# Transposed products in a decoder trunk: two weight blocks at a time, sixteen matmuls with high parts, then sixteen with low parts

## The chip, the cores and the metric

The kernel runs on one core of a Trainium2 chip. Its time is the device time in microseconds (us), lower is better. A core has a matrix engine (PE, or TensorE), VectorE (DVE), ScalarE (ACT), GpSimd (POOL) and SyncE (SP), which in this kernel only issues transfers. The engines run side by side, each through its own row of instructions in order, and wait for one another by semaphores.

## The reference

Two decoder layers over 256 positions of width 2048, all in float32. Layer 0 mixes with a gated DeltaNet, layer 1 with sparse attention; each is followed by a convolutional gated feed-forward part (ffn, width 5120), layer norms and a per-layer embedding.

```
def conv_glu(x, w_gate, w_up, conv_w, w_down):
    gate = causal_dwconv(x @ w_gate, conv_w)
    return (jax.nn.silu(gate) * (x @ w_up)) @ w_down
...
    for i in range(DEPTH):
        if i % N_MIXERS == 0:
            h = gdn_mixer(x, gdn_w_in[ia], gdn_conv_w[ia], ...)
        else:
            h = dsa_mixer(x, dsa_w_in[ib], ...)
        x = layer_norm(DN_ALPHA * x + h, ln1_g[i], ln1_b[i])
        f = conv_glu(x, ffn_w_gate[i], ffn_w_up[i], ffn_conv_w[i], ffn_w_down[i])
        x = layer_norm(DN_ALPHA * x + f, ln2_g[i], ln2_b[i])
        x = x + jax.nn.sigmoid(x @ ple_w_gate[i]) * (p[i] @ ple_w_proj[i])
```

The DeltaNet works in chunks of 64 positions. In each, a triangular matrix made of keys and gates is inverted by forward substitution:

```
    lmat = jnp.where(strict, jnp.einsum('bhncd,bhnsd->bhncs', kb, k) * decay, 0.0)
    amat = lmat + jnp.eye(C, dtype=jnp.float32)
    sol = lax.linalg.triangular_solve(amat, rhs, left_side=True, lower=True, unit_diagonal=True)
```

Nearly all arithmetic is in products of the 256 positions with weight matrices of 2048 or more rows.

## The kernel before

**Products by parts.** PE keeps float32 exactness by splitting every operand in a high part (rounded to the format that PE multiplies in) and a low part (the rest). A product is then high x high, high x low and low x high. The activation is held turned, `xT`: 128 partitions, 16 row blocks, 2 parts, 256 positions. Weights come in blocks of 128 x 1024 elements (512 KB). For each block `weights` (lines 97 to 118) takes a buffer `raw` out of three (pool `wp`), issues its load on SP (line 104), lets ACT copy it into `hi` (line 110) and VectorE subtract into `lo` (line 111). `hi` and `lo` come from the pool `hl`, three buffers each (line 70). Both splits are issued with a priority far ahead, so the scheduler puts them as early as buffers allow.

**Transposed products** (`gemm_t_steps`, lines 120 to 143) have the weights as stationary operand and give their result turned, 128 columns on the partitions. For 256 columns they take two accumulators in PSUM and four blocks. In each block, eight matmuls with high parts (line 133) have high and low parts of the activation side by side as the moving operand (512 wide); then eight with low parts of the weights (line 137) have the high part of the activation alone (256 wide). After each block the generator yields, so that a caller can put other work between blocks; after the last one `done` takes the accumulators. They make the keys, queries and values of the DeltaNet (256 and 512 columns for each of eight groups of four heads; lines 453, 454 and 569), its gates (64 columns: one block of sixteen and sixteen, line 322), gate and up of the ffn (lines 736, 737), and in the sparse layer the index heads, keys and queries (lines 909, 938, 954, 986). The other products (`gemm_steps`, lines 145 to 169) have the activation as stationary operand; all their matmuls move weights (lines 161, 162, 165). They are not touched.

**Group 0 of the DeltaNet** is where other engines' chains matter. Its steps in order:
- the gates' product, turned back by `ab_ps` (line 326); some twenty small steps on VectorE and ACT (lines 328 to 343); `gc_ps` (lines 354 to 356) sums them over a chunk on PE;
- `grow` (line 361): these sums go to memory by POOL's queue; `qd` (line 434): SP loads them back, spread over all partitions; `L` (lines 443, 444): decays, on VectorE;
- `L` times the products of keys (line 513); `lt` (line 518) and `ld` (line 521): SP turns the triangular blocks by way of memory;
- `substitute` (lines 529 to 543): 62 small operations on POOL, then `tt` (line 543) and `pm` (line 557) bring the inverses back in place; `w_ps` (from `mul`, line 549) is PE's first use of them.

`lt` and `ld` share SP's queue with the loads of weights, which wait for `raw` buffers there. The later groups go through the same chain one group ahead, while PE works on products of the group before.

**What sets the order.** A scheduler puts instructions in each engine's row by priority and by what they depend on, from the order in which the program issues them; buffers of a pool are reused in turn.

Of the kernel before, what the change touches and what calls it, by code (L numbers as in the profile page):

```python
# [16 lines left out]
P = 128  # L17
S = 256
D = 2048
KT = D // P  # L20
# [43 lines left out]
class Trunk:  # L64
    def __init__(self, nc, tc, ctx, t):
        self.nc, self.tc, self.t = nc, tc, t
        pool = lambda **k: ctx.enter_context(tc.tile_pool(**k))

        self.const = pool(name="const", bufs=1)
        self.hl = pool(name="hl", bufs=3)  # L70
        self.xtp = pool(name="xtp", bufs=1)
        self.big = pool(name="big", bufs=1)
        self.cp = pool(name="cp", bufs=1, side="right")
        self.wp = pool(name="wp", bufs=3, side="right")
        self.mm = pool(name="mm", bufs=4, space=PSUM)
        self.sp = pool(name="sp", bufs=2, space=PSUM)
        self.dr = pool(name="dr", bufs=2, space=DRAM)
        self.ident = self.const.tile([P, P], F32, tag="ident", name="ident")
        nc.sync.dma_start(out=self.ident, in_=t["cst"][:, C_IDENT:C_IDENT + P])
        cst = self.cst = self.cp.tile([P, N_CONST - P], F32, tag="cst", name="cst")  # L80
        self.tri = cst[:, C_TRI - P:C_TRI - P + P]
        self.cmin = cst[:, C_CMIN - P:C_CMIN - P + P]
        self.xinit = cst[:, C_XINIT - P:C_XINIT - P + 256]
        self.ones = cst[:, C_ONES - P:C_ONES - P + P]
        self.causal = cst[:, C_CAUSAL - P:C_CAUSAL - P + P]
        self.qmin = cst[:, C_QMIN - P:C_QMIN - P + P]
        self.xT = self.xtp.tile([P, KT, 2, S], F32R, tag="xT", name="xT")
        self.behind, self.first = [], ()
# [28 lines left out]
            self.first = ()  # L117
        return hi, lo

    def gemm_t_steps(self, src, c0, n, x, done, kt=KT):  # L120


        nc = self.nc
        for c in range(c0, c0 + n, 256):
            w = min(256, c0 + n - c)
            nt = [(o, min(P, w - o)) for o in range(0, w, P)]
            ps = [self.mm.tile([P, 512], F32, tag="mm", name="mm_ps") for _ in nt]
            nk = 1024 // w
            for k0 in range(0, kt, nk):
                hi, lo = self.weights(src, k0 * P, nk, (c, w))  # L130
                for k in range(nk):
                    for (o, m), q in zip(nt, ps):
                        nc.tensor.matmul(q[:m, :], hi[:, k, o:o + m], x[:, k0 + k].rearrange("p a b -> p (a b)"),  # L133
                                         start=k0 + k == 0, stop=False)
                for k in range(nk):
                    for (o, m), q in zip(nt, ps):
                        self.tail = nc.tensor.matmul(q[:m, S:], lo[:, k, o:o + m], x[:, k0 + k, 0, :],  # L137
                                                     start=False, stop=k0 + k == kt - 1)
                if k0 + nk < kt:
                    yield  # L140
            for (o, m), q in zip(nt, ps):
                done((c - c0 + o) // P, q[:m, :])
            yield
# [38 lines left out]
            steps = [g for g in steps if next(g, steps) is not steps]  # L182

    def gemm_t(self, *args):
        self.go_(self.gemm_t_steps(*args))

    def gemm(self, *args):
        self.go_(self.gemm_steps(*args))
# [209 lines left out]
    def gdn_groups(self, pool, gk, cw, ng, oT, load, taps, gates, ahead):  # L398
# [4 lines left out]
        nc, t = self.nc, self.t  # L403
        w_in = t["gdn_w_in"]
# [10 lines left out]
        def conv(n0, out):  # L415

            def done(n, ps):
                pd = pads[n % 2]
                self.fold(pool, pd[:, 3:], ps)
                ac = pool.tile([P, S], F32, tag="ac", name="ac", bufs=2)  # L420
                w = cw[:, :, n0 + n]
                nc.scalar.activation(ac, pd[:, 3:], AF.Identity, scale=w[:, 3:4])
                for k in (2, 1, 0):
                    nc.vector.scalar_tensor_tensor(ac, pd[:, k:k + S], w[:, k:k + 1], ac, op0=ALU.mult, op1=ALU.add)
                o = out(n)
                nc.scalar.activation(o, ac, AF.Tanh, scale=0.5)
                nc.vector.scalar_tensor_tensor(o, o, 1.0, ac, op0=ALU.add, op1=ALU.mult)
            return done
# [19 lines left out]
        def keys(g, rest=()):  # L448

            s = {"g": g}  # L450
            q = s["q"] = pool.tile([P, 2, S], F32, tag="q", name="q")
            k = s["k"] = pool.tile([P, 2, S], F32, tag="k", name="k")
            steps = (self.gemm_t_steps(w_in, 2048 + 256 * g, 256, self.xT, conv(16 + 2 * g, lambda n: k[:, n])),
                     self.gemm_t_steps(w_in, 256 * g, 256, self.xT, conv(2 * g, lambda n: q[:, n])))
            if not g:

                for nb in range(4):
                    load(nb, self.tail if nb else None)
                    if nb:
                        next(steps[1])  # L460
                    if nb == 3:
                        taps(self.tail)
                    self.first = self.halves
                    next(steps[0])
                next(steps[1])
                gates()
            for x in steps:
                for _ in x:
                    if rest:
                        rest.pop(0)()  # L470
            return s
# [180 lines left out]
        def front(s):  # L652
            decays(s)
            sums(s)
            blocks(s)

        n, rest = keys(0), []
        front(n)
        substitute(n)
        for g in range(8):  # L660
            s = n
            rest += values(s)
            if g:
                zgate(s, rest)
                rest = []
            else:
                zgate(s, [])
            if g < 7:
                n = keys(g + 1, rest)
            else:  # L670
                ahead()
            inverses(s)
            if g < 7:
                front(n)
                substitute(n)
            solve(s)
            rest = outputs(s)
# [29 lines left out]
    def ffn(self, i, affine):  # L707
        nc, tc, t = self.nc, self.tc, self.t
        with tc.tile_pool(name="hp", bufs=1) as hp, tc.tile_pool(name="fp", bufs=1) as pool:
            NF = D_FF // P  # L710
            hT = self.parted(hp, "hT", NF)
            cw = self.fcw
            gates = {}
            pads = [pool.tile([P, 2 + S], F32, tag=f"fpd{i}", name=f"fpd{i}") for i in range(2)]
            for pd in pads:
                nc.gpsimd.memset(pd[:, 0:2], 0.0)

            def gate(n, ps):
                pd = pads[n % 2]
                self.fold(pool, pd[:, 2:], ps)  # L720
                ac = gates[n] = pool.tile([P, S], F32, tag="fac", name="fac", bufs=3)
                nc.scalar.activation(ac, pd[:, 2:], AF.Identity, scale=cw[:, 2, n:n + 1])
                for k in (1, 0):
                    nc.vector.scalar_tensor_tensor(ac, pd[:, k:k + S], cw[:, k, n:n + 1], ac,
                                                   op0=ALU.mult, op1=ALU.add)
                self.mark = nc.scalar.activation(ac, ac, AF.Silu)

            def up(n, ps):
                h = pool.tile([P, S], F32, tag="fh", name="fh", bufs=2)
                self.fold(pool, h, ps)  # L730
                nc.vector.tensor_tensor(h, h, gates[n], op=ALU.mult)
                self.split(hT(n)[:, 0], hT(n)[:, 1], h)

            distances = self.distances(pool) if not i else iter(())
            for n in range(0, NF, 2):
                steps = (self.gemm_t_steps(t["ffn_w_gate"][i], n * P, 256, self.xT, lambda m, ps: gate(n + m, ps)),
                         self.gemm_t_steps(t["ffn_w_up"][i], n * P, 256, self.xT, lambda m, ps: up(n + m, ps)))
                if n:
                    for x in steps:
                        self.go_(x)  # L740
                else:
                    self.go_(*steps)
                if n % 4 == 0:
                    next(distances, None)
                if n in (6, 14, 22, 30):
                    affine(pool, n // 8, self.mark)()
            return self.project(pool, t["ffn_w_down"][i], hT, NF, t["ln2_g"][i], t["ln2_b"][i], lambda: self.fill)
# [300 lines left out]
```

## Time and profile before

| what | value |
|---|---|
| three runs | 2846.52, 2847.19, 2851.07 us |
| median | 2847.19 us |
| span of the profiled execution, first to last instruction | 2843.5 us |
| ACT's splits (line 110), 929 of them | 977.8 us, 1053 ns each |
| loads over the span | 513.94 MB read, 183 GB/s |
| POOL's substitution, both lines, 248 operations each | 116.2 + 115.5 us |

The profiled execution has only its span; its own time is not recorded apart from the runs, whose median lies 3.7 us above it. Busy times are those of the engine's instructions; a matmul is given with its drain, so successive ones overlap, and the pace of PE is read from the distance of starts. In the list of waits, a row gives who waited for whom, total us, how many times, and the longest. In a timeline, a row gives start and length in us, engine, line, operation, tiles, shapes, how many instructions are drawn together, and in brackets the idle time before and its releaser. In a row of windows, the figures are the window's length, busy time and instructions of PE, PE's weight loads, DVE, ACT and POOL, the granted clock of PE, and the share and rate of transfers.

### The profile page before, as it was taken

Reading aid. Unit: us, or ns where it says so; the run is one execution under the profiler, and the core shown is the slowest. Engines: PE = TensorE matmul, PEld = TensorE weight load, DVE = VectorE, ACT = ScalarE, POOL = GpSimd, SP = SyncE. Lnnn points to the kernel's source line nnn. Section 1 sums busy time; section 2 is a strip of 40 time slices with the busy share of each in tenths; the row PEclk is TensorE's granted clock in tenths of the full one; section 3 lists DMA queues with packets and bytes.
Section 4 is the critical chain, followed back from the end, with each engine's and each line's share of the span. In section 5 each row is a group of like instructions: output and inputs, shape, how many; then the busy total and the mean of one; then the engine's idle time right before and its main releaser. Section 6 shows DMA issues by size and latency. Waiting matters only on the chain. (4 is left out here: it accounts for less than half of the span.)

```text
span 2843.5 us, 40202 instructions
## 1 busy us (share of the span) xinstructions
PE 2801.9 (99%) x15022; PEld 2405.1 (85%) x15022; DVE 1852.0 (65%) x3026; ACT 1402.9 (49%) x2187; POOL 346.8 (12%) x688
## 2 busy tenths in 40 slices
PE   9799999999999999999999999999999999999999
PEld 7688888888887888888888789888888888888877
DVE  6578777788555666666554665665576666655566
ACT  4455555555434555555433454455365555543354
POOL 1433344432300000000000000120000000000000
PEclk9899999999999999999999999999999999999999
DMA  6655656655565666666655666654556666656556
GB/s 203 154 136 160 164 163 172 168 159 150 165 217 174 185 199 202 202 207 202 195 192 193 193 190 198 194 151 143 192 171 196 197 193 193 195 191 193 193 185 200
DMA packets 411796, 520.83 MB, mean 183 GB/s; under 512 B 28460, under 2 KB 301232, under 8 KB 411344
## 3 DMA queue, kind: packets, MB, share of 16 engines
q1 hardware_dynamic: 404432, 499.91, 58.1%
q0 software_dynamic: 7168, 18.35, 2.7%
q8 instruction: 118, 1.93, 0.3%
q14 instruction: 78, 0.64, 0.1%
HBM read 513.94 MB, written 7.39 MB: 183 GB/s over the span
## 5 line engine op out<-in xcount | busy, mean ns | idle before, releaser
L111 DVE TENSOR_TENSOR lo<-raw,hi 128x1024 fp32r<-128x1024 f32 (+1 forms) x929 | 1135.3, 1223 | 792.6 <-ACT hi L110 770.4
L110 ACT ACTIVATE hi<-raw 128x1024 fp32r<-128x1024 f32 (+1 forms) x929 | 977.8, 1053 | 1178.5 <-PE mm_ps L133 473.6
L133 PE MATMUL mm_ps<-xT,hi 128*128 128x512 f32 (+1 forms) x4176 | 1065.7, 395 | 2.7 <-ACT hi L110 2.7
L133 PEld LDWEIGHTS mm_ps<-xT,hi 128*128 128x128 f32 (+1 forms) x4176 | 750.5, 189 | 136.1 <-ACT hi L110 3.3
L137 PEld LDWEIGHTS mm_ps<-xT,lo 128*128 128x128 f32 (+1 forms) x4176 | 573.7, 190 | 40.9
L137 PE MATMUL mm_ps<-xT,lo 128*128 128x256 f32 (+1 forms) x4176 | 596.9, 284 | 0.0
L161 PE MATMUL b_ps<-hi,xT 128*128 128x512 f32 (+1 forms) x704 | 272.7, 389 | 0.6 <-DVE xT L302 0.4
L162 PE MATMUL b_ps<-hi,xT 128*128 128x512 f32 (+1 forms) x704 | 269.4, 384 | 0.0
L161 PE MATMUL b_ps<-hi,hTA 128*128 128x512 f32 x512 | 199.4, 390 | 0.0
L162 PE MATMUL b_ps<-hi,hTA 128*128 128x512 f32 x512 | 199.2, 389 | 0.0
L165 PE MATMUL b_ps<-lo,xT 128*128 128x512 f32 (+1 forms) x704 | 189.1, 383 | 0.0
L538 POOL TENSOR_TENSOR xt<-ld,xi 128x60 f32<-128x60 f32 (+24 forms) x248 | 116.2, 468 | 356.8 <-DMA ld<-lt 338.0
L161 PEld LDWEIGHTS b_ps<-hi,xT 128*128 128x128 f32 x704 | 132.2, 188 | 24.7 <-DVE xT L302 0.7
L162 PEld LDWEIGHTS b_ps<-hi,xT 128*128 128x128 f32 x704 | 132.6, 188 | 23.5
L165 PEld LDWEIGHTS b_ps<-lo,xT 128*128 128x128 f32 x704 | 130.1, 188 | 24.7
L214 POOL DMA_DIRECT2D lng<-in_ln_g x16 | 8.7, 545 | 1134.7 <-ACT hi L110 598.2
L165 PE MATMUL b_ps<-lo,hTA 128*128 128x512 f32 x512 | 136.9, 389 | 0.0
L540 POOL TENSOR_TENSOR xi<-xi,xt 128x60 f32<-128x60 f32 (+24 forms) x248 | 115.5, 466 | 19.4
L165 PEld LDWEIGHTS b_ps<-lo,hTA 128*128 128x128 f32 x512 | 96.1, 188 | 20.0
L161 PEld LDWEIGHTS b_ps<-hi,hTA 128*128 128x128 f32 x512 | 96.1, 188 | 19.9
L162 PEld LDWEIGHTS b_ps<-hi,hTA 128*128 128x128 f32 x512 | 96.1, 188 | 19.8
L161 PE MATMUL b_ps<-hi,oT 128*128 128x512 f32 x256 | 100.4, 392 | 0.0
(260 smaller groups left out, 2519.7 us busy)
## 6 DMA issues: line engine op xcount, KB each, us to landing
raw<-in_gdn_w_in SPq DMA_DIRECT2D x193, 512.0 KB, 4.0
raw<-in_ffn_w_gate SPq DMA_DIRECT2D x160, 512.0 KB, 4.0
raw<-in_ffn_w_up SPq DMA_DIRECT2D x160, 512.0 KB, 3.6
raw<-in_ffn_w_down SPq DMA_DIRECT2D x160, 512.0 KB, 3.7
raw<-in_dsa_w_in SPq DMA_DIRECT2D x72, 512.0 KB, 3.6
raw<-in_gdn_w_o SPq DMA_DIRECT2D x64, 512.0 KB, 4.3
raw<-in_ple_w_gate SPq DMA_DIRECT2D x64, 512.0 KB, 4.9
raw<-in_dsa_w_o SPq DMA_DIRECT2D x32, 512.0 KB, 3.7
```

Of the source, the lines that this page charges most:

```text
L110: act = nc.scalar.activation(hi, raw, AF.Copy)
L111: ins = nc.vector.tensor_tensor(lo, raw, hi.bitcast(F32), op=ALU.subtract)
L133: nc.tensor.matmul(q[:m, :], hi[:, k, o:o + m], x[:, k0 + k].rearrange("p a b -> p (a b)"), start=k0 + k == 0, stop=False)
L137: self.tail = nc.tensor.matmul(q[:m, S:], lo[:, k, o:o + m], x[:, k0 + k, 0, :], start=False, stop=k0 + k == kt - 1)
L161: nc.tensor.matmul(ps[a][:, :n], xh, hi[:, k, :], start=k0 + k == 0, stop=False)
L162: nc.tensor.matmul(ps[a][:, :n], xl, hi[:, k, :], start=False, stop=False)
L165: self.last = nc.tensor.matmul(ps[a][:, :n], x(k0 + k)[:, 0, a * P:(a + 1) * P], lo[:, k, :], start=False, stop=k0 + k == kt - 1)
L214: ins = self.nc.gpsimd.dma_start(out=r, in_=bass.AP(tensor=src.tensor, offset=src.offset, ap=[[0, P], [1, n]]))
L538: nc.gpsimd.tensor_tensor(tmp[:, :m, :w], bcast(ld[:, i + 1:, i], m, 1), xi[:, :m, i:i + 1].to_broadcast([P, m, w]), op=ALU.mult)
L540: nc.gpsimd.tensor_tensor(xi[:, :m, i + 1:], xi[:, :m, i + 1:], tmp[:, :m, :w], op=ALU.subtract)
```

## The change

`gemm_t_steps` gets a parameter `run`: so many blocks are prepared at once, then all their matmuls with high parts are issued, then all with low parts, and the generator yields after that. With `run=2` this is sixteen and sixteen. `gemm_t` always passes 2; the two callers that use the steps directly pass 2 save for the first group of the DeltaNet and the first columns of each ffn; the index heads of the sparse layer (line 909 of before) keep 1. `hi` and `lo` get a fourth buffer. The additional 8 KB of each partition are taken from the scratch area of software-issued transfers, 8192 bytes in place of the default 16384. The number of instructions of each kind stays as it was; 492 of the 520 blocks of eight and eight are paired.

```diff
-        self.hl = pool(name="hl", bufs=3)
+        self.hl = pool(name="hl", bufs=4)
...
-    def gemm_t_steps(self, src, c0, n, x, done, kt=KT):
+    def gemm_t_steps(self, src, c0, n, x, done, kt=KT, run=1):
...
-            for k0 in range(0, kt, nk):
-                hi, lo = self.weights(src, k0 * P, nk, (c, w))
-                for k in range(nk):
-                    for (o, m), q in zip(nt, ps):
-                        nc.tensor.matmul(q[:m, :], hi[:, k, o:o + m], x[:, k0 + k].rearrange("p a b -> p (a b)"),
-                                         start=k0 + k == 0, stop=False)
-                for k in range(nk):
-                    for (o, m), q in zip(nt, ps):
-                        self.tail = nc.tensor.matmul(q[:m, S:], lo[:, k, o:o + m], x[:, k0 + k, 0, :],
-                                                     start=False, stop=k0 + k == kt - 1)
-                if k0 + nk < kt:
+            for b0 in range(0, kt, nk * run):
+                parts = [(k0, *self.weights(src, k0 * P, nk, (c, w))) for k0 in range(b0, min(b0 + nk * run, kt), nk)]
+                for k0, hi, _ in parts:
+                    for k in range(nk):
+                        for (o, m), q in zip(nt, ps):
+                            nc.tensor.matmul(q[:m, :], hi[:, k, o:o + m], x[:, k0 + k].rearrange("p a b -> p (a b)"),
+                                             start=k0 + k == 0, stop=False)
+                for k0, _, lo in parts:
+                    for k in range(nk):
+                        for (o, m), q in zip(nt, ps):
+                            self.tail = nc.tensor.matmul(q[:m, S:], lo[:, k, o:o + m], x[:, k0 + k, 0, :],
+                                                         start=False, stop=k0 + k == kt - 1)
+                if b0 + nk * run < kt:
                     yield
...
-        self.go_(self.gemm_t_steps(*args))
+        self.go_(self.gemm_t_steps(*args, run=2))
...
+            run = 2 if g else 1
...
+            steps = (self.gemm_t_steps(w_in, 2048 + 256 * g, 256, self.xT, conv(16 + 2 * g, lambda n: k[:, n]), run=run),
+                     self.gemm_t_steps(w_in, 256 * g, 256, self.xT, conv(2 * g, lambda n: q[:, n]), run=run))
...
+                run = 2 if n else 1
...
-    nc = bacc.Bacc("TRN2", target_bir_lowering=False, num_devices=1)
+    nc = bacc.Bacc("TRN2", target_bir_lowering=False, num_devices=1, dynamic_dma_scratch_size=8192)
```

Lines of the changed kernel stand one to four further down than before (133 is 134, 137 is 139, 326 is 328, 354 is 356, 513 is 516, 518 is 521); 104, 110 and 111 stay.

How this moves work in the rows of the engines, at three places. First PE, in group 0, from the high parts ahead of the turned gates (ab_ps) to the sums gc_ps; in the change the low parts of the gates' product, 64 columns wide, are shown as well, and in before a block of eight and eight stands between them and the first row. Before:

```order
L133 MATMUL mm_ps<-xT,hi 128x512 x3
L326 MATMUL ab_ps<-ident,gates 128x64 x2
L133 MATMUL mm_ps<-xT,hi 128x512 x5
L137 MATMUL mm_ps<-xT,lo 128x256 x8
L133 MATMUL mm_ps<-xT,hi 128x512 x8
L137 MATMUL mm_ps<-xT,lo 128x256 x8
L133 MATMUL mm_ps<-xT,hi 128x512 x8
L137 MATMUL mm_ps<-xT,lo 128x256 x8
L133 MATMUL mm_ps<-xT,hi 128x512 x8
L137 MATMUL mm_ps<-xT,lo 128x256 x8
L133 MATMUL mm_ps<-xT,hi 128x512
L354 MATMUL gc_ps<-gates,cst 128x64
```

In the change:

```order
L139 MATMUL mm_ps<-xT,lo 64x256 x16
L134 MATMUL mm_ps<-xT,hi 128x512 x12
L328 MATMUL ab_ps<-ident,gates 128x64 x2
L134 MATMUL mm_ps<-xT,hi 128x512 x4
L139 MATMUL mm_ps<-xT,lo 128x256 x16
L134 MATMUL mm_ps<-xT,hi 128x512 x16
L139 MATMUL mm_ps<-xT,lo 128x256 x16
L134 MATMUL mm_ps<-xT,hi 128x512 x16
L139 MATMUL mm_ps<-xT,lo 128x256 x16
L134 MATMUL mm_ps<-xT,hi 128x512 x8
L356 MATMUL gc_ps<-gates,cst 128x64
```

Between ab_ps and gc_ps stood 30 high and 32 low matmuls; now 44 and 48 do. Second VectorE, at the last steps of the gates just ahead of gc_ps (L340 to L343 of before are L342 to L345 of the change; ac and pd belong to the convolution of the values). Before:

```order
L340 SCALAR_TENSOR_TENSOR gates<-gates 128x64
L196 TENSOR_TENSOR pd_105<-mm_ps,fold 128x256
L342 SCALAR_TENSOR_TENSOR gates<-gates 128x64
L343 SCALAR_TENSOR_TENSOR gates<-gates 128x64
L111 TENSOR_TENSOR lo<-raw,hi 128x1024
L357 COPY gc<-gc_ps 128x64
```

In the change:

```order
L342 SCALAR_TENSOR_TENSOR gates<-gates 128x64
L426 SCALAR_TENSOR_TENSOR ac<-pd_104,cw,ac 128x256
L344 SCALAR_TENSOR_TENSOR gates<-gates 128x64
L426 SCALAR_TENSOR_TENSOR ac<-pd_104,cw,ac 128x256
L111 TENSOR_TENSOR lo<-raw,hi 128x1024 x2
L345 SCALAR_TENSOR_TENSOR gates<-gates 128x64
L429 SCALAR_TENSOR_TENSOR v<-v,ac 128x256
L426 SCALAR_TENSOR_TENSOR ac<-pd_105,cw,ac 128x256
L359 COPY gc<-gc_ps 128x64
```

The splits of a pair now stand together, ahead of the last step of the gates. Third SP's queue in group 0, from the weight loads before qd to ld. Before:

```order
L104 DMA raw<-in_gdn_w_in 128x2x512 x3
L434 DMA qd<-grow 128x2x512
L104 DMA raw<-in_gdn_w_in 128x2x512
L434 DMA qd<-grow 128x2x512
L104 DMA raw<-in_gdn_w_in 128x2x512 x4
L518 DMA lt<-L 32x8x32 x4
L104 DMA raw<-in_gdn_w_in 128x4x256
L521 DMA ld<-lt 128x1x1024
```

In the change:

```order
L104 DMA raw<-in_gdn_w_in 128x2x512 x5
L436 DMA qd<-grow 128x2x512 x2
L104 DMA raw<-in_gdn_w_in 128x2x512 x3
L104 DMA raw<-in_gdn_w_in 128x4x256 x2
L521 DMA lt<-L 32x8x32 x4
L104 DMA raw<-in_gdn_w_in 128x4x256
L524 DMA ld<-lt 128x1x1024
```

Eight loads of weights stood ahead of lt from the first row on; now ten do. From group 1's lt on the number is the same in both (24 from one lt to the next), and VectorE's last step of L (line 513) stands behind two splits where it stood behind one.

More of the change, by code (lines that the diff above doesn't have):

```diff
@@ L452, in keys @@
             k = s["k"] = pool.tile([P, 2, S], F32, tag="k", name="k")
-            steps = (self.gemm_t_steps(w_in, 2048 + 256 * g, 256, self.xT, conv(16 + 2 * g, lambda n: k[:, n])),
-                     self.gemm_t_steps(w_in, 256 * g, 256, self.xT, conv(2 * g, lambda n: q[:, n])))
+            run = 2 if g else 1
+            steps = (self.gemm_t_steps(w_in, 2048 + 256 * g, 256, self.xT, conv(16 + 2 * g, lambda n: k[:, n]), run=run),
+                     self.gemm_t_steps(w_in, 256 * g, 256, self.xT, conv(2 * g, lambda n: q[:, n]), run=run))
             if not g:
@@ L735, in ffn @@
             for n in range(0, NF, 2):
-                steps = (self.gemm_t_steps(t["ffn_w_gate"][i], n * P, 256, self.xT, lambda m, ps: gate(n + m, ps)),
-                         self.gemm_t_steps(t["ffn_w_up"][i], n * P, 256, self.xT, lambda m, ps: up(n + m, ps)))
+                run = 2 if n else 1
+                steps = (self.gemm_t_steps(t["ffn_w_gate"][i], n * P, 256, self.xT, lambda m, ps: gate(n + m, ps), run=run),
+                         self.gemm_t_steps(t["ffn_w_up"][i], n * P, 256, self.xT, lambda m, ps: up(n + m, ps), run=run))
                 if n:
```

## Prediction

> **What bounds the kernel now.** I read the page first, then PE's list of waits, then timelines of PE in an undisturbed stretch and at the one long wait.
>
> ```profile
> PE 2801.9 (99%) x15022; PEld 2405.1 (85%) x15022; DVE 1852.0 (65%) x3026; ACT 1402.9 (49%) x2187; POOL 346.8 (12%) x688
> PEclk9899999999999999999999999999999999999999
> L111 DVE TENSOR_TENSOR lo<-raw,hi 128x1024 fp32r<-128x1024 f32 (+1 forms) x929 | 1135.3, 1223 | 792.6 <-ACT hi L110 770.4
> L133 PE MATMUL mm_ps<-xT,hi 128*128 128x512 f32 (+1 forms) x4176 | 1065.7, 395 | 2.7 <-ACT hi L110 2.7
> L137 PE MATMUL mm_ps<-xT,lo 128*128 128x256 f32 (+1 forms) x4176 | 596.9, 284 | 0.0
> ```
>
> PE is busy 2801.9 of 2843.5 us, at full granted clock nearly throughout. The two lines that the change groups hold 1065.7 and 596.9 us, with 2.7 and 0.0 us of idle time before them: the weights always arrive in time. VectorE, which makes the low parts, idles 792.6 us before them. So only two things can move the time: the pace at which PE issues matmuls, and its waits.
>
> ```profile
> PE w_ps L549 <- DMA pm<-tt: 19.0, 1, 19.0
> PE n_ps L293 <- ACT xb L299: 5.5, 6, 1.1
> PE mm_ps L133 <- ACT hi L110: 2.7, 2, 1.7
> ```
>
> In PE's list of waits (total, times, longest), half of all waiting is one event of 19.0 us. Here it is in PE's timeline (start, length, line, count), with the windows' row of the ten microseconds behind it:
>
> ```profile
> 119.34 1.11 PE L137 MATMUL mm_ps<-xT,lo 128*128 128x256 f32 x8
> 139.41 3.70 PE L549 MATMUL w_ps<-pm,L 128*128 128x96 f32 x16 [18.96 <-DMA pm<-tt]
> 139.00:149.00 10.00, 9.59 (x39) 9.12 (x40) 4.20 (x13) 2.38 (x9) 0.00 (x0) 0.51 0.01 2
> ```
>
> In group 0 of the DeltaNet layer PE has nothing left to do until the inverse of the triangular blocks comes back; the clock then stands at 0.51 for these ten microseconds. This has a consequence for every sum below: what PE gains or loses before 120 us vanishes in that hole, while a delay of the chain that ends it shifts everything behind it one for one.
>
> **The pace: what grouping removes.** In PE's timeline of the first ffn, a block is a run of eight high-part matmuls and a run of eight low-part ones:
>
> ```profile
> 1001.13 2.00 PE L133 MATMUL mm_ps<-xT,hi 128*128 128x512 f32 x8
> 1002.98 1.12 PE L137 MATMUL mm_ps<-xT,lo 128*128 128x256 f32 x8
> 1003.21 0.88 PE L137 MATMUL mm_ps<-xT,lo 128*128 128x256 f32 x6
> 1003.93 2.00 PE L133 MATMUL mm_ps<-xT,hi 128*128 128x512 f32 x8
> 1005.77 1.11 PE L137 MATMUL mm_ps<-xT,lo 128*128 128x256 f32 x8
> 1006.72 2.00 PE L133 MATMUL mm_ps<-xT,hi 128*128 128x512 f32 x8
> ```
>
> (The third row is the end of the run above it, from a narrower window.) Lengths overlap, so the distances of starts count: 1.84 us for eight high parts (1003.93 to 1005.77), 0.95 for eight low ones, 2.79 for a block. Is the first high run after low parts slower than a later one? The other products, whose moving side is always 512 wide, tell. The rows are the first and fourth-but-last starts of three successive high runs:
>
> ```profile
> 72.18 0.40 PE L161 MATMUL b_ps<-hi,xT 128*128 128x512 f32 x1
> 74.02 1.07 PE L165 MATMUL b_ps<-lo,xT 128*128 128x512 f32 x4
> 74.92 0.39 PE L161 MATMUL b_ps<-hi,xT 128*128 128x512 f32 x1
> 76.74 1.07 PE L165 MATMUL b_ps<-lo,xT 128*128 128x512 f32 x4
> ```
>
> The eight high matmuls behind 256-wide low parts take 1.84 us (72.18 to 74.02); the next eight, behind 512-wide ones, 1.82. So coming out of a 256-wide run costs about 0.02 us. Against it stands a small loss: the last six of a low run take 0.72 us (1003.21 to 1003.93), 0.120 each, so that eight at this pace need 0.96 where a run from its start needs 0.95: the first two are cheaper, and a run of sixteen has such a start once instead of twice. Net, 0.01 to 0.02 us per pair. Unrounded, the same starts give 25 ns less 8 ns; I take **17 ns**. The diff turns 492 blocks into 246 pairs (32 in the values of the DeltaNet layer, 28 in its keys, 152 in both ffn, 34 in the sparse layer). 246 x 0.017 = **-4.2 us**; bounds from the rows' rounding, -2.5 and -4.9.
>
> The Trainium skill, "TensorE: Matmul & The Clock Gate", section "Back-to-back issue gap", speaks against even this: it gives the gap of an isolated warm matmul by its width alone, N/2.4 ns plus 2.5, so that an order of the same matmuls would change nothing. The trace is above that figure (about 216 ns at 512 by the page, 1.84/8 = 230 ns here) and depends on what came before, 1.84 against 1.82; by the page this term would be 0.
>
> **The chain that ends the hole.** Group 0's chain in before: gates (ab_ps, then VectorE), gc_ps, grow to memory and back as qd, L, lt, ld, POOL's substitution, tt, pm, w_ps.
>
> ```profile
> 45.36 0.33 PE L326 MATMUL ab_ps<-ident,gates 64*128 64x64 f32 x2 [0.30 <-DVE gates L196]
> 56.40 0.23 DVE L343 SCALAR_TENSOR_TENSOR gates<-gates 128x64 f32<-128x64 f32 x1
> 56.69 0.43 PE L354 MATMUL gc_ps<-gates,cst 128*128 128x64 f32 x2
> 58.92 0.62 POOL L361 DMA_DIRECT2D grow<-gates  x1 [35.24 <-DVE gates L359]
> 61.61 0.37 SPq L434 DMA_DIRECT2D qd<-grow  x1
> 71.11 0.48 DVE L443 TENSOR_SCALAR L<-qd,gc 128x128 f32<-128x128 f32 x2
> 80.10 1.12 DVE L513 SCALAR_TENSOR_TENSOR L<-g_ps,c,L 128x128 f32<-128x128 f32 x4
> 81.24 1.82 SPq L518 DMA_DIRECT2D lt<-L  x4
> 97.91 0.25 POOL L538 TENSOR_TENSOR xt<-ld,xi 128x31 f32<-128x31 f32 x1 [38.37 <-DMA ld<-lt]
> 135.38 2.33 POOL L557 DMA_DIRECT2D pm<-tt  x4 [1.87 <-DMA tt<-xi]
> ...
> 160.92 5.20 SPq L104 DMA_DIRECT2D raw<-in_gdn_w_in  x2
> ```
>
> ab_ps waits for the fold of the gates in both kernels, so it stays at 45.36. Between it and gc_ps the order of before puts 30 high and 32 low matmuls; the order of the change puts 44 and 48, since the low parts of a pair come late and gc_ps stands inside the third pair. 14 x 0.23 + 16 x 0.12 = 5.1 us: gc_ps at 61.8. VectorE's last gate step, behind two low-part splits of 1.22 us in the new order, ends at about the same time. grow and qd's issue follow by the same distances: 64.1 and 66.8. Most of this is then taken back. Between qd's issue and the first use of qd at 71.11 lie 9.5 us; its transfer needs only this of them:
>
> ```profile
> DMA to landing us min/median/max: 4.9/5.2/6.2
> ```
>
> so qd lands at 71.7 to 73.0, one split stands beside it, and the first use is at about 73, +1.9. From there to the last L513 three splits stand in between in before and three in the change. But SP's queue differs: lt stands behind two weight loads more than before, each of which waits for a split three blocks earlier; the last of these splits stands between the L513 of the change, and its high part needs a buffer, freed one block earlier with four buffers than with three. That puts lt at 82.7 to 84. I take **+2.5 us** on the chain; the 57 us from lt to pm hold the same instructions. Bounds: 0 (the slack swallows it all) and +10.3 (all of 5.1, and two more loads ahead of lt at the 5.2 us that two take in the last row above, ahead of group 1's lt). PE's own shift before the hole is free.
>
> **Later groups.** Here the chain ends before PE asks:
>
> ```profile
> 224.05 2.32 POOL L557 DMA_DIRECT2D pm<-tt  x4 [3.46 <-PE mm_ps L133]
> 230.01 1.92 PE L549 MATMUL w_ps<-pm,L 128*128 128x96 f32 x16
> ```
>
> In group 1 pm is issued by 226.4 and lands 1.7 us later (137.7 to 139.4 in group 0): 1.9 us to spare, and POOL itself waited 3.46 us for PE. In the new order the last L of a group stands behind two splits (+1.2 us on VectorE), but w_ps also stands further behind in PE's order. I take 0; bounds 0 and +6, if most groups came 3 us too late.
>
> **The rest.** Fourth buffers for hi and lo only let splits run earlier; they were in time already (0.0 us before L137), so 0. The smaller DMA scratch touches the software queue alone, where a few small transfers stand at a time: 0. In a pair the second block's high part is needed 0.95 us earlier than now; VectorE and ACT have the room shown above, and the pair before it gives 3.7 us of high parts as lead, so 0. At layer norms and attention the order puts two splits at once ahead of a cast that PE waits for; the row of n_ps (5.5 us over 6 waits) is the nearest price: two splits 1.22 us longer would add 1 to 2 us, a cast put earlier would gain as much. I take 0, bounds -2 and +3.
>
> **Sum:** -4.2 + 2.5 + 0 = -1.7 us on the span of 2843.5, so 2841.8. The median of the runs, 2847.19, is 3.7 above the span of the profiled execution, which I add: **2845.5 us**, -0.06%. About 0.2% (5.7 us) is what a measurement of this kernel can tell from no change: faster is below 2841.5, slower above 2852.9.
>
> **The rivals.**
> - *Width alone sets the pace.* Grouping then does nothing, and only the chain counts: 2847.2 + 2.5 = 2849.7. For it: the 0.02 us are two units of the view's rounding. Against: they recur at every run. 0.10. It is what the Trainium skill's page gives.
> - *Long low runs go faster.* A block of the same two runs of sixteen exists already, with 64 columns of weights:
>
> ```profile
> 35.93 3.83 PE L133 MATMUL mm_ps<-xT,hi 128*64 128x512 f32 x16
> 39.60 1.98 PE L137 MATMUL mm_ps<-xT,lo 128*64 128x256 f32 x16
> 41.42 2.00 PE L133 MATMUL mm_ps<-xT,hi 128*128 128x512 f32 x8
> ```
>
>   3.67 + 1.82 = 5.49 us, against 2 x 2.79 = 5.58 for a pair. If the length of the runs made this, 246 pairs would gain 22 us: 2847.2 - 22 + 2.5 = 2828. Against it: its sixteen high parts take 3.67, no less than 2 x 1.84 less 0.01, and low parts with 128 columns do not quicken along their run (0.120 at its end). Half as many weight columns explain the rest. 0.05.
> - *The chain of group 0 passes on its whole delay* (slower). Place: SP's queue between qd and lt, and VectorE's splits ahead of L. Price: +10.3, so 2847.2 - 4.2 + 10.3 = 2853.3; with later groups late as well, up to 2859. It decides from 9.9 us of delay at w_ps. For it: 5.1 us are certain up to gc_ps. Against: 9.5 us lie between qd's issue and use where 5 are needed. 0.12.
> - *The small waits add up* at layer norms, attention and later groups: +5 to +7 over the forecast, 2850 to 2852.9. 0.08.
>
> **How the numbers follow.** Forecast 2845.5, reaching from 2839 (transition at its upper bound, chain at 0, small waits at -2) to 2850: 0.65, of which 0.17 lie below 2841.5. With the rivals: faster 0.17 + 0.05 = 0.22; slower 0.12; within 0.2% the other 0.66. The range 2839 to 2853 leaves out the fast rival and most of the slow one.
>
> **What would show it.** In PE's timeline of the ffn a pair should take 5.57 us: sixteen high parts 3.66, sixteen low ones 1.91. 5.49 means the second rival, 5.59 the first. The wait of w_ps should end near 142, with gc_ps near 61.8 and lt at 82.7 to 84; over 149 is the slow rival. The waits list should hold no new w_ps entry from later groups, and no hi or lo as releaser beyond some 3 us. I am wrong if PE starves for a pair's second block, or if runs of sixteen have a pace of their own that runs of eight do not show.

## The result, and the profile after

The changed kernel takes 2867.12 us (median of four runs, 2863.02 to 2870.15), the kernel before 2848.77 in runs beside it: a ratio of 1.0062, 95% interval 1.005 to 1.0075. Forecast was 0.9994, with a range that ended at 2853. The profiled execution has a span of 2862.7 us, 19.2 more than that of before.

First the page's line of busy times, then PE's list of waits (who waits for whom, total us, times, longest):

```profile
PE 2795.5 (98%) x15022; PEld 2401.1 (84%) x15022; DVE 1843.9 (64%) x3026; ACT 1408.2 (49%) x2187; POOL 347.9 (12%) x688
PE w_ps L552 <- DMA pm<-tt: 24.6, 2, 22.7
PE ot_ps L643 <- DVE ot L637: 15.5, 8, 3.2
PE mm_ps L134 <- ACT hi L110: 4.0, 3, 2.1
```

PE is busy 6.4 us less than before, so the matmuls did become quicker; it idles more. One row is new: `ot_ps`, the turn of the DeltaNet's outputs, waits 15.5 us for VectorE, once in each of eight groups. In before the same wait was 0.2 us in all, in the last group alone, where the change leaves it as it was:

```profile
PE ot_ps L640 <- DVE ot L634: 0.2, 1, 0.2
```

Two steps that the prediction did work out came as worked out. PE's timeline in the first ffn shows the pair at 5.57 us (1004.07 to 1009.64), 3.66 of high parts and 1.91 of low:

```profile
1004.07 3.82 PE L134 MATMUL mm_ps<-xT,hi 128*128 128x512 f32 x16
1007.73 2.08 PE L139 MATMUL mm_ps<-xT,lo 128*128 128x256 f32 x16
1009.64 3.82 PE L134 MATMUL mm_ps<-xT,hi 128*128 128x512 f32 x16
```

And the chain of group 0, in the timelines of PE and SP, has gc_ps at 62.05 (61.8 forecast), lt at 82.83 (82.7 to 84), w_ps at 141.06, 1.65 later than before (2.5 forecast):

```profile
62.05 0.43 PE L356 MATMUL gc_ps<-gates,cst 128*128 128x64 f32 x2
82.83 1.82 SPq L521 DMA_DIRECT2D lt<-L  x4
141.06 3.70 PE L552 MATMUL w_ps<-pm,L 128*128 128x96 f32 x16 [22.68 <-DMA pm<-tt]
```

Counted from the first use of one group's inverses to the next (w_ps), groups 1 to 6 took 85.5 to 86.1 us each in before; now they take 87.9 to 90.4. From group 0's w_ps to group 7's the changed kernel needs 627.1 us, 20.8 more; from there to the end 2094.5, 3.3 less. So the loss stands in the DeltaNet layer, between w_ps and w_ps.

**One such wait followed back.** PE's timeline of group 1 (the groups count from 0):

```profile
273.43 0.39 PE L625 MATMUL o_ps<-u,qd 128*128 128x128 f32 x2
...
290.19 0.66 PE L643 MATMUL ot_ps<-ident,ot 128*128 128x128 f32 x4 [3.05 <-DVE ot L637]
```

From the last products of the outputs (o_ps) to their turn PE has 13.7 us of other work and 3.05 of waiting. In before it was 13.5 us and no wait, so PE's own row is as long as it was:

```profile
267.49 0.39 PE L622 MATMUL o_ps<-u,qd 128*128 128x128 f32 x2
...
281.00 0.60 PE L640 MATMUL ot_ps<-ident,ot 128*128 128x128 f32 x4
```

What stands between on VectorE are the sums of squares (`of`), an inverse root by three rounds of small steps (`rs`, `rt`), and the scaling (`ot`). In before, group 1, in parts:

```profile
269.58 0.16 DVE L626 SCALAR_TENSOR_TENSOR of<-oss,wq 128x4 f32<-128x4 f32 x1 [1.67 <-ACT sqs L625]
270.82 1.21 DVE L111 TENSOR_TENSOR lo<-raw,hi 128x1024 fp32r<-128x1024 f32 x1
273.78 0.35 DVE L634 SCALAR_TENSOR_TENSOR ot<-o_ps,rs,zs 128x128 f32<-128x128 f32 x1
274.94 1.39 DVE L111 TENSOR_TENSOR lo<-raw,hi 128x1024 fp32r<-128x1024 f32 x1 [0.81 <-ACT hi L110]
276.25 1.38 DVE L634 SCALAR_TENSOR_TENSOR ot<-o_ps,rs,zs 128x128 f32<-128x128 f32 x5
```

The fourth `ot`, which releases the first turn, is done at 277.1, 3.9 us before PE asks for it. That is its slack. After, group 1:

```profile
275.28 2.47 DVE L111 TENSOR_TENSOR lo<-raw,hi 128x1024 fp32r<-128x1024 f32 x2 [1.58 <-PE mm_ps L139]
277.67 0.25 DVE L629 SCALAR_TENSOR_TENSOR of<-oss,wq 128x4 f32<-128x4 f32 x1
...
281.77 1.23 DVE L111 TENSOR_TENSOR lo<-raw,hi 128x1024 fp32r<-128x1024 f32 x1 [2.35 <-ACT hi L110]
282.91 0.27 DVE L260 TENSOR_TENSOR rt<-rs 128x8 f32<-128x8 f32 x1
283.11 0.47 DVE L426 SCALAR_TENSOR_TENSOR ac<-pd,cw,ac 128x256 f32<-128x256 f32 x1
...
287.87 0.60 DVE L637 SCALAR_TENSOR_TENSOR ot<-o_ps,rs,zs 128x128 f32<-128x128 f32 x2
288.39 1.22 DVE L111 TENSOR_TENSOR lo<-raw,hi 128x1024 fp32r<-128x1024 f32 x1
289.54 1.37 DVE L637 SCALAR_TENSOR_TENSOR ot<-o_ps,rs,zs 128x128 f32<-128x128 f32 x5
```

And ACT at the same place:

```profile
279.80 0.99 ACT L441 ACTIVATE qo<-qd,go 128x128 f32<-128x128 f32 x3 [2.96 <-DMA qd<-grow]
280.69 1.04 ACT L110 ACTIVATE hi<-raw 128x1024 fp32r<-128x1024 f32 x1
```

Counted from the last o_ps, three things come on top. Two splits of a pair, which wait 1.58 us for PE to free low-part buffers, stand ahead of the second `of`: it comes 4.2 us after the last o_ps instead of 2.1. (ACT's sums end later too, with a split among them; without VectorE's two splits `of` could have come after 2.9.) A split within the inverse root waits 2.35 us for ACT, which stands at the next group's qd (2.96 us, with the high part behind it): it ends at 283.0, 9.6 us after, against 4.5. Behind it, six steps of the values' convolution (line 426) and one more split stand among the rest of the root. The fourth `ot` is ready at 290.1, 16.7 us after the last o_ps instead of 9.6. The 7 us eat the 3.9 of slack, and PE waits for the other 3.

**The wait has a second price.** The windows of PE just behind the waits at 199, 290 and 555 us (the figure before the last two is the granted clock):

```profile
199.20:202.60 3.40, 3.38 (x12) 2.72 (x13) 3.40 (x8) 0.69 (x1) 2.93 (x7) 0.66 0.67 169
290.00:293.40 3.40, 3.21 (x16) 2.71 (x17) 3.40 (x9) 1.31 (x2) 3.00 (x6) 1.00 0.60 161
555.60:559.00 3.40, 3.35 (x11) 2.83 (x12) 3.40 (x8) 0.69 (x1) 2.93 (x7) 0.54 0.61 168
```

After two of the three the granted clock of the window is 0.66 and 0.54, and eleven or twelve matmuls are done where sixteen are after the other. The period with the wait of 2.84 us at 555.6 is 4.4 us longer than in before, 1.5 more than the wait.

### The profile page after: what moved, and what is told of

Same layout as the page of the kernel before. It is cut to its first block, busy times and chain, and to the rows that moved or that the text cites. A ratio compares the mean times of both kernels' runs of the same rounds, so it can differ in the third digit from the quotient of the medians.

```text
span 2862.7 us, 40648 instructions
## 1 busy us (share of the span) xinstructions
PE 2795.5 (98%) x15022; PEld 2401.1 (84%) x15022; DVE 1843.9 (64%) x3026; ACT 1408.2 (49%) x2187; POOL 347.9 (12%) x688
## 5 line engine op out<-in xcount | busy, mean ns | idle before, releaser
L111 DVE TENSOR_TENSOR lo<-raw,hi 128x1024 fp32r<-128x1024 f32 (+1 forms) x929 | 1122.2, 1224 | 782.7 <-ACT hi L110 544.1
L134 PE MATMUL mm_ps<-xT,hi 128*128 128x512 f32 (+1 forms) x4176 | 1026.5, 394 | 4.1 <-ACT hi L110 4.0
L134 PEld LDWEIGHTS mm_ps<-xT,hi 128*128 128x128 f32 (+1 forms) x4176 | 762.4, 189 | 151.0 <-ACT hi L110 5.7
L139 PEld LDWEIGHTS mm_ps<-xT,lo 128*128 128x128 f32 (+1 forms) x4176 | 539.3, 191 | 21.6
L139 PE MATMUL mm_ps<-xT,lo 128*128 128x256 f32 (+1 forms) x4176 | 552.9, 283 | 0.0
L541 POOL TENSOR_TENSOR xt<-ld,xi 128x60 f32<-128x60 f32 (+24 forms) x248 | 122.5, 494 | 378.9 <-DMA ld<-lt 360.1
L167 PE MATMUL b_ps<-lo,hTA 128*128 128x512 f32 x512 | 136.9, 389 | 0.0
```

The source lines that it names most:

```text
L111: ins = nc.vector.tensor_tensor(lo, raw, hi.bitcast(F32), op=ALU.subtract)
L167: self.last = nc.tensor.matmul(ps[a][:, :n], x(k0 + k)[:, 0, a * P:(a + 1) * P], lo[:, k, :], start=False, stop=k0 + k == kt - 1)
L541: nc.gpsimd.tensor_tensor(tmp[:, :m, :w], bcast(ld[:, i + 1:, i], m, 1), xi[:, :m, i:i + 1].to_broadcast([P, m, w]), op=ALU.mult)
```

## The experiments

The theories: **A**, the pairs of the DeltaNet's values put splits ahead of the outputs' scaling on VectorE, and PE waits for it; **B**, the pairs of the keys do it; **C**, the fourth buffer does it, by letting splits run ahead; **D**, the wait only shows a lateness from elsewhere.

**All DeltaNet products single** (pairs in ffn and sparse layer stay):

```diff
-            run = 2 if g else 1
+            run = 1
...
-            self.gemm_t(w_in, 4096 + 512 * g, 512, self.xT, conv(32 + 4 * g, lambda n: v[:, n]))
+            self.gemm_t(w_in, 4096 + 512 * g, 512, self.xT, conv(32 + 4 * g, lambda n: v[:, n]), run=1)
```

> All DeltaNet products (keys and values of every group) with one block at a time; ffn and sparse layer keep pairs, four buffers. Theory A (the pairs of the DeltaNet's values put splits ahead of the scaling of the outputs on VectorE, and the turn of the outputs, ot_ps, waits for that on PE): ot_ps waits under 0.5 us in all, w_ps of group 0 near 139, span 2839 to 2841, 3 to 4 us below before, since 186 pairs gain 17 ns each. Theory B (the pairs of the keys do it): the same here. Theory C (the fourth buffer alone lets the splits run ahead of the scaling): ot_ps still waits some 15 us, span near 2860.

Its list of waits:

```profile
PE w_ps L552 <- DMA pm<-tt: 21.2, 3, 18.0
PE ot_ps L643 <- DVE ot L637: 0.2, 1, 0.2
```

Ratio to before 0.9999 (0.999 to 1.0008). The wait of ot_ps is gone with four buffers still in place, against C. The span, 2850.3, is ten above what was expected: w_ps of group 0 comes at 141.7 where 139 was expected, w_ps waits in two later groups as well (3.2 us), and the clock is halved behind one of these. So this run alone doesn't show the gain of the pairs.

**Only the values single**, the keys of groups 1 to 7 in pairs (the second half of the diff above):

> Only the DeltaNet's values with one block at a time; keys of groups 1 to 7, ffn and sparse layer keep pairs. Theory A: ot_ps waits under 1 us in all, w_ps of group 0 near 139, span 2838 to 2842. Theory B: ot_ps waits some 15 us, span near 2860. Theory C: the same 15 us.

```profile
PE w_ps L552 <- DMA pm<-tt: 19.2, 1, 19.2
PE ot_ps L643 <- DVE ot L637: 0.2, 1, 0.2
```

Ratio 0.9978 (0.9969 to 0.9987): faster than before, by 0.2%. w_ps of group 0 comes at 141.3, not near 139, and the span, 2843.4, lies 1.4 above the expected range. The order of VectorE's row shows why ot_ps is on time: no split stands between the two `of`, as in before.

**Only the keys single**, values in pairs (the first half of the diff):

> Only the DeltaNet's keys with one block at a time; values, ffn and sparse layer keep pairs. Theory A: ot_ps waits 10 to 16 us in all, w_ps of group 0 near 141, span 2856 to 2863. Theory B: ot_ps does not wait, span near 2842.

```profile
PE w_ps L552 <- DMA pm<-tt: 31.8, 4, 23.3
PE ot_ps L643 <- DVE ot L637: 8.1, 7, 1.9
```

Ratio 1.0058 (1.0045 to 1.0072). ot_ps waits in seven groups, though 8 us rather than 10 to 16. So the time, with a span of 2864.3 just above the expected range, isn't made by ot_ps alone: the later groups' w_ps waits 8.5 us, against 2 in the changed kernel. With the two runs before it this settles A against B for the wait of ot_ps: single values take it away with keys in pairs or single, single keys don't.

**The turns one block later on PE**, VectorE's row unchanged up to the scaling:

```diff
-                if j > 2 and rest:
+                if j > 3 and rest:
```

> The changed kernel, but the four turns of a group (two of outputs, two of values) begin one block of the z product later on PE: the row of VectorE is the same, ot_ps asks some 2.7 us later. Theory A: ot_ps waits 0.5 to 1.5 us in all instead of 15.5, and the span falls by 13 to 16 us, to 2847 to 2850. If the wait of ot_ps is only where another lateness shows (theory D: PE is late for a reason further back, and the time returns at the next wait), the span stays within 3 us of the changed kernel's 2862.7.

```profile
PE w_ps L552 <- DMA pm<-tt: 26.6, 3, 22.7
PE ot_ps L643 <- DVE ot L637: 3.1, 5, 1.4
```

Span 2851.5, 11 below the changed kernel; ratio to before 0.9995 (0.9982 to 1.0009). ot_ps waits 3.1 us, some 2 more than expected, and w_ps 3.9 in later groups. The four turns of a group are all that moves on PE (on VectorE the low parts of the turned outputs follow them, one split later), and the time that the wait took is gained: D falls. By the medians the whole loss is gone.

**The outputs' scaling ahead of splits on VectorE**, all pairs kept (the steps are those of the changed kernel, now issued with priority):

```diff
+                with self.tc.high_priority(offset=2 * W_AHEAD):
+                    nc.vector.scalar_tensor_tensor(f[:, a], ss[:, a], 1.0 / 128, bcast(s["wq"][:, :, a], 2, 2),
+                                                   op0=ALU.mult, op1=ALU.add)
...
+            with self.tc.high_priority(offset=2 * W_AHEAD):
+                fa = self.rsqrt(pool, f.rearrange("p a j r -> p (a j r)"), 8)
...
+                with self.tc.high_priority(offset=2 * W_AHEAD):
+                    for h in h4:
+                        ins = nc.vector.scalar_tensor_tensor(ot[:, h], parts[a][:, h], fa[:, 4 * a + h:4 * a + h + 1],
+                                                             s["zs"][:, a, h * P:(h + 1) * P], op0=ALU.mult, op1=ALU.mult)
```

> The changed kernel, with the scaling of the outputs on VectorE (sums, inverse root, products) given priority over the splits: all pairs stay. Fewer splits stand ahead of the last product (four or two in a group instead of six or four). Theory A: ot_ps waits 1 to 7 us in all instead of 15.5, and the time falls by as much against the changed kernel, to between 0 and 0.4% above before.

```profile
PE ot_ps L646 <- DVE ot L640: 7.8, 6, 2.0
```

Ratio 1.0018 (1.001 to 1.0027), two thirds of the loss back, with half of the wait. The eight `ot` came to stand together and two splits fewer stand ahead of the last of them; the other four are still there, two by the `of`, one in the root and one behind it.

**Four buffers alone**, every block single:

```diff
-        self.hl = pool(name="hl", bufs=3)
+        self.hl = pool(name="hl", bufs=4)
```

(and the smaller scratch area)

> The kernel before, with four buffers for hi and lo and the smaller scratch area, every block single. If the lateness of group 0 (w_ps at 141.1 to 141.7 in all runs with four buffers, 139.4 in the kernel before) comes from the fourth buffer, by way of the order on VectorE, and not from pairs: w_ps of group 0 at 141 to 142 here, ot_ps waits under 0.5 us, time 0 to 0.15% above before. If it comes from pairs: w_ps at 139 to 140 and the time that of before.

```profile
PE w_ps L549 <- DMA pm<-tt: 24.1, 3, 20.4
PE ot_ps L640 <- DVE ot L634: 0.2, 1, 0.2
```

Ratio 1.0005 (0.9995 to 1.0015). No wait of ot_ps. w_ps of group 0 comes at 143.1, a microsecond beyond what was expected, so pairs aren't needed for a late group 0. (The expectation's range for the runs with four buffers leaves out the single keys, at 140.4.)

**Pairs with three buffers**, the changed kernel otherwise:

> The changed kernel with three buffers and the scratch area of before: all pairs stay, the values' too. The order of VectorE's row between the sums of the outputs and their scaling is that of the changed kernel, so by theory A ot_ps waits 10 to 16 us in all and the time is 0.4 to 0.7% above before. If the wait needs the fourth buffer: under 3 us, time within 0.2% of before.

```profile
PE ot_ps L643 <- DVE ot L637: 17.8, 8, 3.3
```

Ratio 1.0097 (1.0081 to 1.0114), slower than expected. The wait is a little longer than with four, and its second price larger: the granted clock is 0.96 to 0.98 in each of five successive windows of 85 to 90 us, where the changed kernel has two such of the five. The wait doesn't need the fourth buffer. w_ps of group 0 comes at 138.9, so all pairs together don't make group 0 late either.

**Values single, three buffers**:

> Values single, keys of groups 1 to 7, ffn and sparse layer in pairs, as in the run of the single values, but with three buffers and the scratch area of before. If the fourth buffer only delays group 0: w_ps of group 0 near 139.4, all else as with four, time 0.2 to 0.35% below before. If pairs need the fourth buffer: PE waits 10 us and more in all for hi or lo (mm_ps), time at or above before.

```profile
136.86 3.70 PE L552 MATMUL w_ps<-pm,L 128*128 128x96 f32 x16 [16.05 <-DMA pm<-tt]
PE mm_ps L134 <- ACT hi L110: 4.2, 2, 2.6
PE b_ps L163 <- ACT hi L110: 1.7, 2, 1.0
```

Ratio 0.9979 (0.997 to 0.9989), 2843.9 us: with the single values and four buffers (0.9978) the fastest version here. Pairs don't need the fourth buffer (6 us of waiting for high parts in all). Group 0 ends earlier than in any other run, 2.5 us ahead of what was expected.

**The kernel before, once more**:

> The kernel before, once more, for its profile: what of the differences between profiles is the same kernel's own variation. In the second ffn, between two fixed matmuls, the same 402.1 us as in the first profile within 0.1; ot_ps under 0.5 us; the waits of w_ps and the windows of half clock in the DeltaNet may differ by some us.

```profile
PE w_ps L549 <- DMA pm<-tt: 25.5, 3, 19.0
PE ot_ps L640 <- DVE ot L634: 0.2, 1, 0.2
```

Its span is 2857.7, 14 above its first profile: the same kernel, with waits of w_ps in two later groups (6.5 us), group 0's w_ps at 140.7, and half clock behind the waits. The wait of ot_ps is 0.2 us again. So ot_ps tells the kernels apart from one profile each, and a w_ps of some microseconds doesn't.

**Four blocks at a time in the ffn**, values single, four buffers:

```diff
-                run = 2 if n else 1
+                run = 4 if n else 1
```

> As the run of the single values, but the ffn takes four blocks at a time (32 matmuls with high parts, then 32 with low). If the gain is a price for each step from low parts to high parts (19 ns for each one removed, from 402.1 to 400.7 us in the second ffn with 76 pairs), it falls once more by half as many steps, 38 x 19 ns = 0.7 us, to 400.0 us, provided that the splits keep up. If long runs have a pace of their own, it falls by more than 1.4 us. If four blocks at once make PE wait for its weights, it rises.

PE's timeline in the second ffn, where it didn't wait, and its row of waits:

```profile
2306.30 7.44 PE L134 MATMUL mm_ps<-xT,hi 128*128 128x512 f32 x32
2313.59 4.00 PE L139 MATMUL mm_ps<-xT,lo 128*128 128x256 f32 x32
2317.42 7.44 PE L134 MATMUL mm_ps<-xT,hi 128*128 128x512 f32 x32
...
PE mm_ps L134 <- ACT hi L110: 15.5, 9, 2.3
```

Four blocks take 11.12 us (2306.30 to 2317.42); two pairs take 11.13 (2301.13 to 2312.26 in the run of the single values with three buffers). Unrounded it is 0.02 once more for the step removed. But PE now waits 15.5 us for high parts, and the ratio is 1.0042 (1.0028 to 1.0056). The pace is a price for each step, not one of long runs.

## Why the prediction was wrong

**The pace was right.** Between the same two matmuls of the second ffn, 144 blocks or 72 pairs apart (not 76, as the expectation of the fours has it), the trace has 402.12 us in both profiles of before and with four buffers alone, and 400.68 in every run with the ffn in pairs and four buffers: 1.44 us, 20 ns per pair, against 17 forecast. It is the one term that comes out alike in all these runs; with three buffers half a microsecond of it is lost (401.17 and 401.27). The two rivals about the pace (nothing, or 22 us) fall.

**The chain of group 0 was right in its times, but not in its cause.** gc_ps and lt came as forecast, w_ps 1.65 later against 2.5. But the delay was put down to the pairs, and it goes with the fourth buffer (and the smaller scratch area, always changed with it), of which the prediction said: "Fourth buffers for hi and lo only let splits run earlier; they were in time already (0.0 us before L137), so 0". In all eight runs with four buffers, pairs or not, gc_ps comes at 59.6 to 62.8 and 27 loads of weights stand ahead of group 0's lt; in the four with three buffers, the one with all pairs among them, gc_ps comes at 56.7 to 58.3 and 25 or 26 loads stand there. What reaches w_ps is small: 139.5 to 143.2 with four buffers, 136.9 to 140.7 with three, and the kernel before alone gave 139.4 and 140.7. That the forecast of this term came close is in part luck.

**The step that failed** is "The rest": in a pair "VectorE and ACT have the room shown above", and elsewhere "I take 0, bounds -2 and +3". This last names layer norms and attention alone; the turn of the DeltaNet's outputs has no term, so it was put at nothing without a reason. The step took VectorE's 792.6 us of idle time as cover. But VectorE is a row in order, and the question is what stands ahead of the steps that PE waits for. The order of the changed kernel showed it: two splits in front of the second `of`, and four more among the steps behind, for the outputs of each group but the last. In before, three splits stood between the second `of` and the last `ot`; the turn had 3.9 us of slack in group 1 (2.4 to 4.4 in all groups but the last), and the prediction didn't ask for it: a wait that doesn't occur has no row in the list of waits. What the runs showed in place of this 0: 15.3 us more of waiting at ot_ps, some 2.5 for the clock behind two of the waits, and 2 at w_ps in the last group. With +1.65 for group 0 and -3.3 behind the DeltaNet this makes 18.2 of the 19.2. How much of the 15.3 is due to splits and how much to the convolution's steps between them was not separated.

**The slow rival had the wrong place.** It was put at 2853 and at the chain through SP; its decision point, w_ps of group 0 past 149, was never reached. "The small waits add up" named the later groups, at 5 to 7 us; their one wait alone took double.

**The time of before** was read 1.9 us too generously: the changed kernel's profiled run took 2864.45 us with a span of 2862.7, so about 1.75 lie around a span, and the other 2 of the 3.7 were a profile quicker than the median. The lower end of the range has a slip as well: 4.9 and 2 us below 2847.2 make 2840.3, not 2839.

**Why the version with single values beats before** is shown only in part. The 214 pairs that it keeps are worth some 4 us at 20 ns. It is 6 us faster (0.9978), and 5 us faster than with all DeltaNet products single too, while 28 pairs of keys account for 0.6. In its profile ld is issued 3.1 to 3.2 us after lt (groups 1 to 7); with keys and values single, as in before, it is 4.9 to 5.3, and with the keys alone single 6.7 to 6.8. In its profile only group 0's w_ps waits; with the products single, and in before's second profile, later groups' w_ps do too, and most with the keys alone single. That this slack on the substitution is the rest was not tested by itself. Besides, a group in which nothing waits takes 85.7 us in it and 86.0 in before, 2 us over all groups, four times what the pairs of keys explain; why is open.

## What to carry to other kernels

Where a change moves work in an engine's row, take each place where the critical engine depends on that row, also those with no wait in the profile, and put its slack (when the result is ready, and when it is asked for) beside what now stands ahead of it. Idle time of an engine as a sum is no cover: here 792.6 idle microseconds didn't cover 15.5 of waiting. Grouping may then be kept where nobody waits behind it, and left out where a chain shares the row.

## What the runs showed of the hardware

Behind a wait of PE of some 2 to 3 us the granted clock sometimes falls to half and sometimes doesn't: in the changed kernel it did after 3.17 and 2.84 us, and didn't after 3.05 (windows above). The stretch at half clock lasts 3.41 us there. It can be twice as long, and it can come after a shorter wait: in the second profile of before it came after 1.55 us:

```profile
405.32 0.88 PE L549 MATMUL w_ps<-pm,L 128*128 128x96 f32 x6 [1.55 <-DMA pm<-tt]
406.50:413.30 6.80, 6.80 (x29) 6.40 (x28) 4.21 (x14) 2.34 (x9) 0.00 (x0) 0.50 0.26 77
```

The period behind it, without another wait, took 89.4 us instead of 86.0: 3.4 us lost to the clock, twice the wait itself. In the changed kernel the clock cost 1 to 1.5 us a time. So equal waits give unequal times.

A high-part run of 512 wide matmuls takes about 28 ns more when it follows a run of 256 wide ones: between two low runs, eight take 1841 ns, sixteen 3654 and thirty-two 7281 (medians of before, the changed kernel and the fours). Against this the start of a low run saves 8 ns (952, 1913 and 3833 ns). That leaves 20 ns for a step removed, 1.44 us over 72 pairs, and as much again for each where pairs became fours.
